# A higher rank for the softplus of stick breaking in a two-layer hybrid trunk

## The chip, the cores and the metric

The kernel runs on one core of one Trainium2 chip. The metric is the device time of one execution in microseconds (us); the time before is the median of three runs. A profile of one more execution gives the start and the duration of every instruction.

## The reference, cut

A trunk of two layers on 512 tokens of 1024 features, in f32. Each layer normalises its input, projects it with one wide matrix, runs five attention branches on pieces of the projection, gates and merges their outputs, projects once more and adds the residual. The branch that the change touches is stick breaking, four heads of 64:

```python
def _stick_breaking_attention(q, k, v):
    ...
        z = jnp.einsum('bqhd,bshd->bhqs', q_blk, k).astype(jnp.float32) * scale
        strict = (s_pos[None, :] < t[:, None])[None, None]
        log_keep = jnp.where(strict, jax.nn.log_sigmoid(-z), 0.0)
        later = lax.cumsum(log_keep, axis=3, reverse=True) - log_keep
        a = jnp.where(strict, jnp.exp(jax.nn.log_sigmoid(z) + later), 0.0).astype(v.dtype)
        return jnp.einsum('bhqs,bshd->bqhd', a, v)
```

The logarithm of the sigmoid of −z is minus the softplus of z, so the kernel forms softplus(z) = max(z, 0) + ln(1 + exp(−|z|)) for every pair of positions, sums it over later keys and subtracts the sum from z before one last exponential. The other branches: sparse attention with an index score and a top-k (A), forgetting attention (B), native sparse attention (D) and attention into 256 memory tokens (E).

## The kernel before, in words

Features lie on the 128 partitions, tokens along the free axis. TensorE (PE) computes every f32 product as three products of split numbers: `split` (lines 291 to 295) makes a high part `hi` by a copy on ScalarE (ACT) and the rest `lo` by a subtraction on VectorE (DVE), and `mm3` multiplies hi·hi, hi·lo and lo·hi. A projection of 128 output features over 512 tokens takes 24 matmuls into one bank `pj`. Its weights come in pieces of 128 x 1024 numbers: `load` has SyncE (SP) fetch one into `wraw` (two buffers), `wload` splits it into `whi` (line 294, ACT) and `wlo` (line 295, DVE), three buffers each. There are 183 such splits; one piece serves one projection.

The order of the work: Python generators are interleaved by `weave`, which gives every instruction a place in the program. When the kernel is built, a scheduler sets each engine's list: of the instructions that its own model of the time takes to be ready it picks the one of the highest rank. The rank is the place in the program, less an offset where the code stands in `tc.high_priority(offset=...)`. Loads and splits of weights stand in `early()`, with an offset of 3000; everything else of the stages told of here had none. On the chip every engine runs its list in order and waits at an instruction until what it needs is there.

Stick breaking is `sb_attn(pr)` (line 1005), called in each layer for two pairs of heads. A pair has two heads `e` and four blocks of keys `j` = 3, 2, 1, 0 with 128, 256, 384 and 512 columns of queries, so there are 8 passes per call and 32 in all. One pass is:

- `begin`: two matmuls of `Ks` and `Qs` and a mask of `sbm` form z in a PSUM bank `sbz` (tag "T" for even `j`, "S" for odd; the index scores `S` use "S" too). ACT makes |z| (line 1030), its exponential and the logarithm of one more (`lnexp`, line 428); DVE makes `sp_t` = max(z, 0) + that (line 1033).
- `middle`, of the pass before: matmuls with `nones` and `ntri` (matrices of −1, full and triangular) add the sums of softplus of later keys into the bank of z: `nones` for later blocks, `ntri` for the block itself, each for the high and the low half of `sp`. They write over what line 1033 reads. Then ACT forms `sb_a`, the last exponential.
- `store`: DVE puts `sp_t` as a high half (line 1049, CAST) and a low half (line 1050, TENSOR_TENSOR) into `sp`.

After the 8 passes 16 products of `sb_a` and the values fill a bank `Yc` (PE). `sb_attn(0)` is woven with the projections for the silu gate of this branch, the index keys and the memory (lines 1458 and 1462); `sb_attn(1)` (line 1465) with the memory queries, the index scores of branch A (`S`, `R` on line 930, `score` on line 931, `Qi` on lines 920 and 921), the gate of branch E (`G`, `Z`) and the first two parts of branch D's projections. Behind it comes the memory attention, woven with merges and the top-k of `score` (lines 976 and 977). In the profiled execution layer 0's two calls lie at about 56 to 98 and 107 to 152 us, layer 1's at 696 to 751 and 758 to 803 us.

Of the kernel before, what the change touches and what calls it, by code (L numbers as in the profile page):

```python
# [14 lines left out]
AF = mybir.ActivationFunctionType  # L15
OP = mybir.AluOpType
# [173 lines left out]
def trunk(ctx: ExitStack, tc: tile.TileContext, xt, memt, pos, wall, small, vec, ca, cb, out):  # L190
    nc = tc.nc
    dep_info = mybir.DependencyInfo(mybir.DependencyClass.NoSync, mybir.DependencyReason.DATA)

    def after(ins, *earlier):
        for e in earlier:
            if e is not None:
                tc.add_manual_dep(ins.ins, e.ins.name, dep_info, reason="issue order")
# [13 lines left out]
    def slot(name, dt=F32, shape=(128, 512)):  # L211
        return st.tile(list(shape), dt, name=name, tag="st")

    def bank(name, tag, shape=(128, 512)):
        return ps.tile(list(shape), F32, name=name, tag=tag, bufs={"pj": 3, "S": 2, "T": 3}[tag])
# [40 lines left out]
    ones1 = const.tile([128, 1], F32, name="ones1")  # L256
# [22 lines left out]
    def mm(out_, lhsT, rhs, start, stop, **kw):  # L279
        return nc.tensor.matmul(out_, lhsT, rhs, start=start, stop=stop, **kw)  # L280
# [10 lines left out]
    def split(raw, hi, lo, scale=None):  # L291

        if scale is None:
            nc.scalar.activation(hi, raw, AF.Copy)  # L294
            nc.vector.tensor_sub(lo, raw, hi.bitcast(F32))  # L295
        else:
            nc.scalar.activation(hi, raw, AF.Copy, scale=scale)
            nc.vector.scalar_tensor_tensor(lo, raw, scale, hi.bitcast(F32), op0=OP.mult, op1=OP.subtract)
# [128 lines left out]
    def lnexp(*a, **k):  # L427
        i = nc.scalar.activation(*a, **k)
        after(i, state["set"])
        state["ln"].append(i)  # L430
        return i
# [57 lines left out]
    f32 = lambda ap: ap.bitcast(F32)  # L489
# [188 lines left out]
    def y_tiles():  # L678
        a = wk.tile([128, 2, T], F32R, name="yhi", tag="yhi", bufs=2)
        b = wk.tile([128, 2, T], F32R, name="ylo", tag="ylo", bufs=2)  # L680
        return a, b
# [63 lines left out]
    def layer(l, xs, begin):  # L745
# [259 lines left out]
        def sb_attn(pr):  # L1005
            SPW = [512, 384, 256, 256]
            if pr == 0:
                sp = big.tile([128, 6, T], F32R, name="sp", tag="xa")
                lv.SP = [[sp[:, 2 * min(j, 2) + s, 256 * (j == 3):256 * (j == 3) + SPW[j]] for s in range(2)] for j in range(4)]
                for s in range(2):  # L1010
                    nc.vector.memset(f32(lv.SP[3][s][:, 0:128]), 0.0)
            SP = lv.SP
            out = {}

            held = wk.tile([128, 1280], F32, name="sb_a", tag="sb_a", bufs=1)
            first_a = [held[:, 0:512], held[:, 512:896], held[:, 896:1152], held[:, 1152:1280]]

            def begin(e, j):

                h = 2 * pr + e  # L1020
                n, w = SPW[j], T - 128 * j
                ks = slice(128 * j, 128 * j + 128)
                z = bank("sbz", "S" if j % 2 else "T")[:, :n]
                mm(z, lv.KC[h][:, ks], lv.QC[h][:, T - n:], True, False)
                mm(z, lv.KlC[h][:, ks], lv.QC[h][:, T - n:], False, False)
                mw = n - w + 128
                mm(z[:, :mw], identb, sbm[:, 256 - mw:], False, True)
                zw = z[:, n - w:]
                t = wk.tile([128, T], F32, name="sp_t", tag="P", bufs=4)[:, :w]
                nc.scalar.activation(t, zw, AF.Abs)  # L1030
                lnexp(t, t, AF.Exp, scale=-1.0)
                lnexp(t, t, AF.Ln, bias=ones1)
                nc.vector.scalar_tensor_tensor(t, zw, 0.0, t, op0=OP.max, op1=OP.add)
                return e, j, z, t

            def middle(e, j, z, t):

                n = SPW[j]
                for jj in range(3, j - 1, -1):
                    for s in range(2):  # L1040
                        mm(z[:, n - SPW[jj]:], ntri if jj == j else nones, SP[jj][s], False, jj == j and s == 1, skip_group_check=True)
                w = T - 128 * j
                a = first_a[j] if e == 0 else wk.tile([128, T], F32, name="sb_a", tag="PT", bufs=5)[:, :w]
                lnexp(a, z[:, n - w:], AF.Exp)
                out[e, j] = a

            def store(e, j, z, t):
                shi, slo = (x[:, SPW[j] - (T - 128 * j):] for x in SP[j])
                nc.vector.tensor_copy(shi, t)
                nc.vector.tensor_sub(slo, t, f32(shi))  # L1050

            one = None
            for e in range(2):
                for j in (3, 2, 1, 0):
                    new = begin(e, j)
                    if one:
                        middle(*one)
                    store(*new)
                    one = new
                    yield  # L1060
            middle(*one)

            Y = bank("Yc", "T")
            last = None
            for j in (0, 1, 2, 3):
                for e in (1, 0):
                    h = 2 * pr + e
                    m = mm(Y[64 * e:64 * e + 64, 128 * j:], lv.VC[:, j, 64 * h:64 * h + 64], out[e, j], j == 0, j == 3, skip_group_check=True)
                    after(m, last)
                    last = m  # L1070
            if pr == 0:
                lv.YC = y_tiles()
            y = slot("yC")
            nc.vector.tensor_mul(y, Y, lv.ZC[0][:, pr])
            split(y, lv.YC[0][:, pr], lv.YC[1][:, pr])
# [433 lines left out]
```

## Time and profile before

| what | value |
|---|---|
| runs before | 1328.40, 1328.65, 1328.89 us; median 1328.65 |
| the profiled execution's own time | 1326.02 us |
| its span, first to last instruction | 1324.2 us |
| granted clock of TensorE, mean of the span | 0.998 |
| busy: PE / DVE / ACT / POOL | 98% / 69% / 51% / 3% |
| instructions | 18915 |
| chain that ended last | PE 70%, DVE 6%, ACT 5%, issue 2% of the span |
| one `whi` (x183) / one `wlo` (x183), mean | 1058 / 1222 ns |
| line 1033, shortest / median / longest of 32 | 277 / 486 / 694 ns |
| line 1050, shortest / median / longest of 32 | 283 / 487 / 694 ns |

"Busy" is the time in which an engine has at least one instruction running; instructions overlap at their ends, so the time from one start to the next is often shorter than a duration. The chain that ended last is followed backwards from the last instruction, at each step to what released it. A wait in brackets behind a row is idle time of the engine just before that instruction, with the releaser.

### The profile page before, as it was taken

What the parts mean: (1) busy time and instruction counts of PE and PEld (TensorE: products, weight loads), DVE (VectorE), ACT (ScalarE), POOL (GpSimd) and SP (SyncE); (2) the same over time, 40 slices, a digit from 0 to 9 for tenths busy, and PEclk for the clock granted to TensorE, in tenths of its full rate; (3) what the DMA queues carried; (4) which work ended last, traced back from release to release, by engine and by line L of the source; (5) the groups of instructions that cost most, each with busy time, mean ns of one, the idle gap of its engine ahead of it and who ended that gap; (6) DMA issues with size and microseconds to landing.
All of it is one profiled execution on the core that took longest, in us unless ns stands there. A gap on an engine that the chain in (4) does not pass through costs nothing.

```text
span 1324.2 us, 18915 instructions
## 1 busy us (share of the span) xinstructions
PE 1300.6 (98%) x7171; PEld 1064.8 (80%) x7171; DVE 914.0 (69%) x1969; ACT 678.2 (51%) x1269; POOL 41.8 (3%) x60
## 2 busy tenths in 40 slices
PE   9999999999999999999999999999999999999997
PEld 7777787887888888888887777778878878888897
DVE  7987999777755556545567699996686564564554
ACT  7877835356544434434447695534484453343341
POOL 0000111000000000000000001110000000000000
PEclk9999999999999999999999999999999999999999
DMA  6442322222222222134523313212122222223231
GB/s 225 135 144 64 117 83 63 90 66 74 72 80 89 79 80 70 58 112 133 181 84 127 97 63 128 80 64 96 48 89 64 87 81 76 86 78 112 96 112 64
DMA packets 40523, 124.10 MB, mean 94 GB/s; under 512 B 4464, under 2 KB 6512, under 8 KB 40432
## 3 DMA queue, kind: packets, MB, share of 16 engines
q1 hardware_dynamic: 40288, 122.63, 28.4%
q8 instruction: 56, 0.92, 0.3%
q10 hardware_dynamic: 144, 0.26, 0.1%
q14 instruction: 35, 0.29, 0.1%
HBM read 118.16 MB, written 4.72 MB: 93 GB/s over the span
## 4 chain that ended last, share of the span: by engine, by line
PE 70%; DVE 6%; ACT 5%; issue 2%; DMA 1%; POOL 0%; DVEq 0%; ACTq 0%
PE pj L280 59%; PE Y L280 4%; PE S L280 3%; PE pt L596 3%; ACT whi L294 1%; DVE wlo L295 1%; DMA mraw<-in_memt_dram 1%; DMA wraw<-in_wall_dram 1%; ACT sw L470 1%; DVE score L977 1%; ACT sw L471 0%; PE sbz L280 0%; DVE m L976 0%; ACT Qi L920 0%; DVE rt L473 0%
## 5 line engine op out<-in xcount | busy, mean ns | idle before, releaser
L280 PE MATMUL pj<-h_hi,whi 128*128 128x512 f32 x1088 | 432.3, 398 | 1.3 <-DVE rt L473 1.0
L280 PE MATMUL pj<-h_lo,whi 128*128 128x512 f32 x1088 | 428.5, 394 | 0.0
L280 PE MATMUL pj<-h_hi,wlo 128*128 128x512 f32 x1088 | 428.1, 394 | 0.0
L294 ACT ACTIVATE whi<-wraw 128x1024 fp32r<-128x1024 f32 x183 | 193.5, 1058 | 333.8 <-PE pj L280 170.3
L295 DVE TENSOR_TENSOR wlo<-wraw,whi 128x1024 fp32r<-128x1024 f32 x183 | 223.6, 1222 | 190.1 <-ACT whi L294 171.5
L280 PEld LDWEIGHTS pj<-h_hi,wlo 128*128 128x128 f32 x1088 | 204.4, 188 | 46.6 <-DVE wlo L295 3.5
L280 PEld LDWEIGHTS pj<-h_hi,whi 128*128 128x128 f32 x1088 | 204.5, 188 | 43.2 <-issue 1.8
L280 PEld LDWEIGHTS pj<-h_lo,whi 128*128 128x128 f32 x1088 | 204.7, 188 | 41.3 <-issue 2.6
L587 ACT ACTIVATE P<-P,nm 128x128 f32<-128x128 f32 (+3 forms) x128 | 71.5, 559 | 77.7 <-DVE nm L586 77.1
L280 PE MATMUL pj<-yhi,whi 128*128 128x512 f32 (+1 forms) x192 | 72.5, 377 | 1.3 <-ACT whi L294 0.5
L586 DVE CUSTOM_DVE_ANT_0 P<-S,CA 128x128 f32<-128x128 f32 (+3 forms) x104 | 48.4, 470 | 36.1 <-PE S L280 35.8
L280 PE MATMUL pj<-ylo,whi 128*128 128x512 f32 (+1 forms) x192 | 71.9, 374 | 0.3 <-DVE ylo L295 0.3
L280 PE MATMUL pj<-yhi,wlo 128*128 128x512 f32 (+1 forms) x192 | 71.9, 374 | 0.0
L596 PE MATMUL pt<-CA,P 128*128 128x128 f32 x384 | 60.2, 274 | 1.7 <-DVE P L635 1.4
L596 PEld LDWEIGHTS pt<-CA,P 128*128 128x128 f32 x384 | 45.6, 141 | 13.0 <-issue 5.2
L434 ACT ACTIVATE G<-pj 128x512 f32<-128x512 f32 x92 | 53.7, 584 | 1.9 <-PE pj L280 1.7
L977 DVE MATCH_REPLACE8 score<-m,score 128x256 f32<-128x256 f32 (+2 forms) x96 | 51.5, 541 | 0.0
L280 PE MATMUL S<-Ks,Qs 128*128 128x256 f32 (+2 forms) x160 | 49.3, 346 | 0.9 <-DVE nm L586 0.9
L976 DVE MAX8 m<-score 128x8 f32<-128x256 f32 (+2 forms) x96 | 49.8, 546 | 0.0
L871 DVE SCALAR_TENSOR_TENSOR G<-G,pj 128x512 f32<-128x512 f32 x64 | 43.6, 681 | 1.3 <-PE pj L280 0.7
L872 DVE TENSOR_TENSOR acc<-acc,G 128x512 f32<-128x512 f32 x64 | 44.0, 687 | 0.7
L280 PEld LDWEIGHTS pj<-yhi,whi 128*128 128x128 f32 x192 | 36.1, 188 | 9.2 <-ACT yhi L294 1.3
(339 smaller groups left out, 2033.2 us busy)
## 6 DMA issues: line engine op xcount, KB each, us to landing
wraw<-in_wall_dram SPq DMA_DIRECT2D x190, 512.0 KB, 3.6
wc<-in_wall_dram SPq DMA_DIRECT2D x16, 256.0 KB, 5.8
x<-in_xt_dram SPq DMA_DIRECT2D x8, 256.0 KB, 5.1
mraw<-in_memt_dram SPq DMA_DIRECT2D x4, 512.0 KB, 4.3
xo<-in_xt_dram SPq DMA_DIRECT2D x8, 256.0 KB, 4.2
xspill<-xn SPq DMA_DIRECT2D x8, 256.0 KB, 2.0
xo<-xspill SPq DMA_DIRECT2D x8, 256.0 KB, 3.1
out_dram<-o SPq DMA_DIRECT2D x8, 256.0 KB, 2.1
```

Of the source, the lines that this page charges most:

```text
L280: return nc.tensor.matmul(out_, lhsT, rhs, start=start, stop=stop, **kw)
L294: nc.scalar.activation(hi, raw, AF.Copy)
L295: nc.vector.tensor_sub(lo, raw, hi.bitcast(F32))
L434: i = nc.scalar.activation(*a, **k)
L470: nc.scalar.activation(sw[a], p[b], AF.Copy)
L586: nc.vector.tensor_tensor_reduce(P, S, mask, -1.0, 3e38, OP.add, OP.min, nm)
L587: nc.scalar.activation(P, P, AF.Exp, bias=nm, scale=-1.0, accum_out=sums)
L596: nc.tensor.transpose(pt[:, 128 * j:128 * j + 128], x[:, c:c + 128], ident)
L871: nc.vector.scalar_tensor_tensor(G, G, gc, p, op0=gop, op1=OP.mult)
L872: nc.vector.tensor_add(acc, acc, G)
L976: nc.vector.max(m8, lv.work[i])
L977: nc.vector.match_replace(lv.work[i], m8, lv.work[i], REPL)
```

## The change

Five instructions of each pass get an offset of 6000, above the 3000 of the weight splits: the exponential and the logarithm on ACT, and lines 1033, 1049 and 1050 on DVE (1034, 1051 and 1052 in the changed file). |z|, `sb_a` and all matmuls keep their rank.

```diff
                 nc.scalar.activation(t, zw, AF.Abs)
-                lnexp(t, t, AF.Exp, scale=-1.0)
-                lnexp(t, t, AF.Ln, bias=ones1)
-                nc.vector.scalar_tensor_tensor(t, zw, 0.0, t, op0=OP.max, op1=OP.add)
+                with tc.high_priority(offset=6000):
+                    lnexp(t, t, AF.Exp, scale=-1.0)
+                    lnexp(t, t, AF.Ln, bias=ones1)
+                    nc.vector.scalar_tensor_tensor(t, zw, 0.0, t, op0=OP.max, op1=OP.add)
...
                 shi, slo = (x[:, SPW[j] - (T - 128 * j):] for x in SP[j])
-                nc.vector.tensor_copy(shi, t)
-                nc.vector.tensor_sub(slo, t, f32(shi))
+                with tc.high_priority(offset=6000):
+                    nc.vector.tensor_copy(shi, t)
+                    nc.vector.tensor_sub(slo, t, f32(shi))
```

No instruction is added or removed, and the lists of SP and POOL are the same as before. The lists of PE, DVE and ACT change in layer 0's two calls and in layer 1's second; in layer 1's first PE's list stays and a few neighbours on ACT and DVE swap. In the stage behind each second call (the memory attention) some of DVE's and PE's rows shift as well. Three places follow. The numbers in names are the program's buffers.

ACT, layer 1, `sb_attn(0)`, the pass of 512 columns (`sp_t_6750`), before:

```order
L428 ACTIVATE sp_t_6750<-sp_t_6750 128x512
L294 ACTIVATE whi_6917<-wraw_6915 128x1024
L517 ACTIVATE Ks_6735<-pj_6709 64x512
L518 ACTIVATE Ks_6735<-pj_6709 64x512
L428 ACTIVATE sp_t_6750<-sp_t_6750,ones1_114 128x512
```

and with the change:

```order
L428 ACTIVATE sp_t_6750<-sp_t_6750 128x512
L294 ACTIVATE whi_6917<-wraw_6915 128x1024
L428 ACTIVATE sp_t_6750<-sp_t_6750,ones1_114 128x512
L517 ACTIVATE Ks_6735<-pj_6709 64x512
L518 ACTIVATE Ks_6735<-pj_6709 64x512
```

The logarithm went from behind two copies to `Ks` to ahead of them; the split of weights stays ahead of it.

DVE, layer 1, `sb_attn(1)`, from the cast of a pass of 512 columns (`sp_t_7268`) to the cast of the next of 128 (`sp_t_7326`), before:

```order
L1049 CAST sp_6548<-sp_t_7268 128x512
L921 TENSOR_TENSOR Qi_7302<-rt1_7204,qhi_7209 32x512
L1050 TENSOR_TENSOR sp_6548<-sp_t_7268,sp_6548 128x512
L463 SCALAR_TENSOR_TENSOR Z_7345<-G_7377,pj_7352 128x512
L931 SCALAR_TENSOR_TENSOR score1_7227<-R_7309,wI_6804,score1_7227 128x256
L931 SCALAR_TENSOR_TENSOR score2_7228<-R_7314,wI_6804,score2_7228 128x384
L934 TENSOR_TENSOR score1_7227<-score1_7227,CA_111 128x128
L295 TENSOR_TENSOR wlo_7628<-wraw_7625,whi_7627 128x1024
L931 SCALAR_TENSOR_TENSOR score3_7229<-R_7319,wI_6804,score3_7229 128x512
L1033 SCALAR_TENSOR_TENSOR sp_t_7326<-sbz_7322,sp_t_7326 128x128
L934 TENSOR_TENSOR score2_7228<-score2_7228,CA_111 128x128
L1049 CAST sp_6548<-sp_t_7326 128x128
```

and with the change:

```order
L1051 CAST sp_6548<-sp_t_7268 128x512
L295 TENSOR_TENSOR wlo_7628<-wraw_7625,whi_7627 128x1024
L1052 TENSOR_TENSOR sp_6548<-sp_t_7268,sp_6548 128x512
L931 SCALAR_TENSOR_TENSOR score1_7227<-R_7309,wI_6804,score1_7227 128x256
L931 SCALAR_TENSOR_TENSOR score2_7228<-R_7314,wI_6804,score2_7228 128x384
L931 SCALAR_TENSOR_TENSOR score3_7229<-R_7319,wI_6804,score3_7229 128x512
L934 TENSOR_TENSOR score1_7227<-score1_7227,CA_111 128x128
L934 TENSOR_TENSOR score2_7228<-score2_7228,CA_111 128x128
L1034 SCALAR_TENSOR_TENSOR sp_t_7326<-sbz_7322,sp_t_7326 128x128
L934 TENSOR_TENSOR score3_7229<-score3_7229,CA_111 128x128
L1051 CAST sp_6548<-sp_t_7326 128x128
```

The split `wlo_7628` went ahead of the low half of `sp` of 512 columns, `Z_7345` behind the cast of 128 columns, and a `Qi` ahead of the stretch.

PE at the same place, before: from the mask of `sbz_7433` to the triangle matmuls of `sbz_7322`, the pass of 128 columns (in a bank of 256):

```order
L280 MATMUL sbz_7433<-sbm_124,identb_123 128x128
L280 MATMUL pj_7514<-h_lo_6455,whi_7510 128x512
L280 MATMUL pj_7514<-h_hi_6454,wlo_7511 128x512
L280 MATMUL pj_7514<-h_hi_6454,whi_7510 128x512
L280 MATMUL pj_7514<-h_lo_6455,whi_7510 128x512
L280 MATMUL pj_7514<-h_hi_6454,wlo_7511 128x512
L280 MATMUL pj_7514<-h_hi_6454,whi_7510 128x512
L280 MATMUL pj_7514<-h_lo_6455,whi_7510 128x512
L280 MATMUL pj_7514<-h_hi_6454,wlo_7511 128x512
L280 MATMUL sbz_7322<-sp_6548,ntri_125 128x256
L280 MATMUL pj_7514<-h_hi_6454,whi_7510 128x512
L280 MATMUL sbz_7322<-sp_6548,ntri_125 128x256
```

and with the change, from the first triangle matmul of `sbz_7264` (512 columns) to the same end:

```order
L280 MATMUL sbz_7264<-sp_6548,ntri_125 128x512
L280 MATMUL sbz_7554<-Qs_6544,Ks_6737 128x512
L280 LDWEIGHTS identb_123
L280 MATMUL sbz_7554<-sbm_124,identb_123 128x128
L280 MATMUL sbz_7433<-Qs_6544,Ks_6735 128x384
L280 MATMUL sbz_7433<-Qs_6544,Ks_6737 128x384
L280 MATMUL sbz_7264<-sp_6548,ntri_125 128x512
L280 LDWEIGHTS identb_123
L280 MATMUL sbz_7433<-sbm_124,identb_123 128x128
L280 MATMUL sbz_7322<-sp_6548,ntri_125 128x256
L280 MATMUL pj_7514<-h_hi_6454,whi_7510 128x512
L280 MATMUL sbz_7322<-sp_6548,ntri_125 128x256
```

The matmuls of `pj_7514` that stood ahead of `sbz_7322`'s first triangle matmul stand behind it; `sbz_7554`, the next pass of 512 columns, is formed earlier.

## Rows read from the trace of the kernel before

**Rows 1.** The page, busy time, share of the span and instructions of each engine
```profile
PE 1300.6 (98%) x7171; PEld 1064.8 (80%) x7171; DVE 914.0 (69%) x1969; ACT 678.2 (51%) x1269; POOL 41.8 (3%) x60
```

**Rows 2.** Waits of PE: what waited <- for what: us in total, times, longest
```profile
PE sbz L280 <- DVE sp_t L1033: 2.5, 4, 1.1
...
PE sbz L280 <- DVE sp L1050: 0.5, 1, 0.5
```

**Rows 3.** Busy time by stretch: stretch, length, PE, PEld, DVE, ACT, POOL, clock, DMA
```profile
56.00:98.00 42.00, 39.85 (x244) 32.65 (x243) 35.42 (x78) 33.30 (x72) 0.00 (x0) 1.00 0.38 122
107.00:152.00 45.00, 44.42 (x216) 33.21 (x215) 42.05 (x79) 42.01 (x79) 0.00 (x0) 1.00 0.19 60
696.00:751.00 55.00, 52.35 (x299) 43.18 (x299) 40.68 (x76) 39.90 (x80) 0.00 (x0) 1.00 0.39 125
758.00:803.00 45.00, 44.43 (x216) 33.23 (x215) 41.97 (x79) 41.95 (x79) 0.00 (x0) 1.00 0.19 59
```

**Rows 4.** Timeline of ACT, layer 1, `sb_attn(0)`: start, us, engine, line, operation
```profile
721.78 0.59 ACT L517 ACTIVATE Ks<-pj 64x512 fp32r<-64x512 f32 x1
...
722.88 0.71 ACT L428 ACTIVATE sp_t<-sp_t,ones 128x512 f32<-128x512 f32 x1
```

**Rows 5.** Timeline of DVE, the same stretch
```profile
721.79 1.22 DVE L295 TENSOR_TENSOR wlo<-wraw,whi 128x1024 fp32r<-128x1024 f32 x1 [1.73 <-ACT whi L294]
723.04 0.69 DVE L496 TENSOR_TENSOR Ks<-pj,Ks 64x512 fp32r<-64x512 f32 x1
723.77 0.69 DVE L1033 SCALAR_TENSOR_TENSOR sp_t<-sbz,sp_t 128x512 f32<-128x512 f32 x1
```

**Rows 6.** Timeline of PE, the same stretch, the wait before it in brackets
```profile
724.52 1.09 PE L280 MATMUL sbz<-sp,nones 128*128 128x256 f32 x6 [1.07 <-DVE sp_t L1033]
```

**Rows 7.** Timeline of PE, layer 0, `sb_attn(0)`, three of its waits
```profile
85.79 0.51 PE L280 MATMUL sbz<-sp,nones 128*128 128x256 f32 x2 [0.53 <-DVE sp_t L1033]
...
87.41 0.39 PE L280 MATMUL pj<-wlo,yhi 128*128 128x256 f32 x1 [0.34 <-DVE wlo L295]
...
95.23 2.38 PE L280 MATMUL Yc<-sb_a,VC 128*64 128x512 f32 x16 [0.42 <-ACT sb_a L428]
```

**Rows 8.** Timeline of DVE, layer 1, `sb_attn(1)`
```profile
780.31 0.68 DVE L1033 SCALAR_TENSOR_TENSOR sp_t<-sbz,sp_t 128x512 f32<-128x512 f32 x1
...
781.57 0.42 DVE L1049 CAST sp<-sp_t 128x512 fp32r<-128x512 f32 x1
782.02 0.69 DVE L921 TENSOR_TENSOR Qi<-rt,qhi 32x512 fp32r<-32x512 f32 x1
...
783.35 0.68 DVE L463 SCALAR_TENSOR_TENSOR Z<-G,pj 128x512 f32<-128x512 f32 x1
...
786.90 0.29 DVE L1033 SCALAR_TENSOR_TENSOR sp_t<-sbz,sp_t 128x128 f32<-128x128 f32 x1
...
787.31 0.22 DVE L1049 CAST sp<-sp_t 128x128 fp32r<-128x128 f32 x1
```

**Rows 9.** Timeline of ACT, the same stretch
```profile
778.92 0.74 ACT L428 ACTIVATE sp_t<-sp_t,ones 128x512 f32<-128x512 f32 x1
...
783.25 0.77 ACT L930 ACTIVATE R<-S 128x256 f32<-128x256 f32 x2 [0.66 <-PE S L280]
...
786.42 0.44 ACT L428 ACTIVATE sp_t<-sp_t,ones 128x128 f32<-128x128 f32 x1
```

**Rows 10.** Timeline of PE, the same stretch
```profile
781.05 1.09 PE L280 MATMUL sbz<-sp,nones 128*128 128x256 f32 x6
781.98 0.40 PE L280 MATMUL pj<-h_lo,whi 128*128 128x512 f32 x1
782.21 0.40 PE L280 MATMUL sbz<-sp,ntri 128*128 128x512 f32 x1
```

**Rows 11.** Timeline of PE, end of layer 1's `sb_attn(1)` and behind it
```profile
794.54 0.39 PE L280 MATMUL S<-KE,Qs 128*128 128x256 f32 x1 [0.25 <-ACT sb_a L428]
...
804.88 0.50 PE L280 MATMUL pj<-h_hi,whi 128*128 128x512 f32 x1 [0.50 <-DVE rt L473]
```

## Prediction

> **What bounds the kernel now.** I read the page first. TensorE (PE) has matmuls running in 1300.6 of 1324.2 us [rows 1], so at most 23.6 us can come from waits, over the whole program. Second, the waits of PE by what they wait for: matmuls into `sbz` stood 2.5 us in four waits for the softplus' last step (`sp_t`, line 1033) and 0.5 us in one for the low half of its stored result (`sp`, line 1050) [rows 2]. These 3.0 us are all that the trace charges directly to the chain that the change raises. Third, the busy time of each engine in the four stretches in which stick breaking runs [rows 3]. They split in two kinds. In the two that weave `sb_attn(0)` with projections PE is idle for 42.00 − 39.85 = 2.15 us (layer 0) and 55.00 − 52.35 = 2.65 us (layer 1), and the two helpers have room (DVE 35.4 of 42 and 40.7 of 55). In the two that weave `sb_attn(1)` PE is idle for only 0.58 and 0.57 us, but DVE and ACT are busy 42.0 of 45 us each: they are almost as full as PE. Removing every idle moment in all four gives 2.15 + 2.65 + 0.58 + 0.57 = 5.95 us; that is the ceiling of any gain made there, 0.45% of the time. Last I read the single rows around the waits, and set the new order beside them.
>
> What can be told from no change is 0.2%, or 2.66 us of 1328.65. The rows come from one execution of 1326.02 us, 2.63 us under the median of the runs shown; I make the sum against it and add 2.63 at the end.
>
> **The change, part by part.** No instruction is added or removed, DMA issues and the orders of SP and POOL stay, so every gain or loss is a wait of PE that goes or comes.
>
> *Layer 1, `sb_attn(0)*: its one long wait, 1.07 us at 724.52 [rows 6]. ACT's new list puts the Ln ahead of two copies to `Ks`. From 721.78 to 722.88 [rows 4] it so comes 1.1 us earlier, and DVE could do `sp_t` at about 722.5. But DVE is in a weight split, `wlo`, from 721.79 to 723.01 [rows 5], which still stands ahead of `sp_t`. So `sp_t` starts at 723.02 in place of 723.77, and the matmuls that clear it 0.75 us earlier. It passes the low half of a `Ks` (0.69 us), which runs behind it now; but the DVE instructions up to the low half of `sp`, for which the next matmuls (`ntri`) wait, are in sum the same as before. The wait moves to them. Bounds: a gain of 1.07 if nothing is late next, nothing if DVE's sum alone decides. I take a gain of 0.1, near the lower bound, because it is their sum that ends last.
>
> The Trainium skill speaks the other way here: Perfetto Trace Analysis, section Optimization Strategy, says to find the gaps on the engine to be kept busy, see which semaphore they wait for, and make that dependency start sooner or end faster, which is what this edit does. By it the 3.0 us of rows 2 would go; by the rows above one third of them goes from one instruction to the next.
>
> *Layer 0, `sb_attn(0)`*: here are waits of 0.53 for `sp_t`, 0.42 for the last exponential ahead of `Yc`, and 0.34 for a `wlo` [rows 7]. The low half of the 384 columns and the `sp_t` of 512 now run ahead of that `wlo`: it comes later by `sp_t` (0.68), the cast (0.42) and that low half (three quarters of some 0.7, 0.5 as an estimate by width) [rows 8], 1.6 us. Bounds: 0.95 gained, 1.6 lost if all of it is a wait. PE's list also moved its uses back, and I take 0, between the two.
>
> *`sb_attn(1)`, both layers*: the term that decides. The stretches of layer 0 and layer 1 are the same to 0.01 us [rows 3] and their lists change alike, so I cost layer 1's and count it twice. In the list of before, eight matmuls of a projection in a row (`pj_7514`, 0.23 us each by the spacing of two starts [rows 10]) stand ahead of the triangle matmuls `ntri` of `sbz_7322`, and before these four others of it. In the new list none is left between the `nones` of `sbz_7264` and these `ntri`: the projection begins behind the first of them. What stays in between is six `nones` (0.93 us to the next start) and about 4350 columns of other matmuls into `sbz` and one into `S`, at 0.23 us for 512, some 1.9 us; 2.8 us in all. The helpers need longer for what these `ntri` wait for, the cast of `sp` with 128 columns:
> - On DVE, before: from `sp_t` 512 at 780.31 to the cast's end at 787.31 + 0.22 = 787.53, 7.22 us. Of that one `Qi` (0.69) and one `Z` (0.68) move out, and one step over 128 columns (as long as `sp_t` 128, 0.29) moves in [rows 8]. 7.22 − 0.69 − 0.68 + 0.29 = 6.1 us. The `wlo` (1.22 [rows 5]) stays inside, and moves ahead of the low half of `sp` 512.
> - On ACT, before: from the Ln of 512 columns at 778.92 to the end of the Ln of 128 columns at 786.42 + 0.44 = 786.86, 7.94 us, with 0.66 idle [rows 9]. In the new list the same instructions stand there but for one Exp of a gate and one Abs less and one copy of 32 rows more; I count 0.2 less for the one that is gone in sum. Without the idle time 7.94 − 0.66 − 0.2 = 7.1 us. Then come `sp_t` 128 and its cast on DVE, 0.41 + 0.22 [rows 8]: the cast ends 7.7 us after that Ln's start.
>
> The `nones` start when the Ln (0.74 [rows 9]) and `sp_t` (0.68 [rows 8]) are through (they write over what it reads), 1.4 us after the Ln's start; PE reaches the `ntri` at 1.4 + 2.8 = 4.2. By ACT it waits 7.7 − 4.2 = 3.5 us; by DVE alone 0.74 + 6.1 − 4.2 = 2.6. I take ACT's, as `sp_t` 128 can't run before that Ln.
>
> Against it: the projection's matmuls are not lost, they stand later and cover later waits. Those are 0.25 at 794.54 and 0.50 at 804.88 [rows 11]. A Yc that comes sooner by what is raised gains at most that much more. 3.5 − 0.25 − 0.50 is 2.75; I take 2.5, the same with a little gained early in the stretch, where raised Ln and `sp_t` pass copies. Bounds per layer: a gain of 0.57, all that is idle there [rows 3], and a loss of 3.5 and one more `wlo` (1.22 [rows 5]) ahead of a projection, 4.7.
>
> Elsewhere the lists differ by a few neighbours, most in the memory attention behind (DVE's passes of the top-k shift); I cost that at nothing, since PE's own list there has merge projections between what it waits for. Without that cover one such swap costs the longer of the two, a split of 1.22 us.
>
> **Sum.** −0.1 + 0 + 2 × 2.5 = +4.9 us; 1326.02 + 4.9 = 1330.9, and against the median 1328.65 + 4.9 = 1333.5 us.
>
> **Rivals.**
> *The waits go, faster (chance 0.16).* Mechanism: the raised Ln and `sp_t` of `sbz_7264` come so much earlier against PE's list that the 7 us of helpers' work lie under the projection ahead of the `nones`, and not behind it. It decides at one point: that `sp_t` must end over 3.5 us before PE gets to the `nones`. Then the 3.0 us of rows 2 and part of the idle of rows 3 are gained: 1328.65 − 3.0 = 1325.6, and no lower than 1328.65 − 5.95 = 1322.7. For it: these instructions are ranked over everything else that the helpers do. Against: ACT has one idle moment of 0.66 in 7.9 us [rows 9], so an earlier Ln puts off the copies to `R`, for which PE waits too.
> *The wait only moves, no change (0.27).* As at 724.52: the gain of one instruction is the delay of its neighbour, and the projections moved back cover as much later as they lose now. 1328.65 + 0 to 2: 1329. For it: at 794 to 805 there are waits to be covered [rows 11]. Against: those that are left sum to 0.75.
> *Splits come late as well (0.07).* Each time a Ln with its Exp, or `sp_t` and its cast (0.68 + 0.42), pass a `whi` or a `wlo`, PE's projection could wait for it. With the bound of 4.7 in both layers: 1328.65 + 9.4 = 1338.0. Only 0.34 of such a wait is in the rows of before [rows 7].
> That the edit does nothing is out: PE's list changes in all of `sb_attn(1)` and in layer 0's `sb_attn(0)`.
>
> **How the numbers follow.** The forecast, a loss in both `sb_attn(1)`, has 0.50: the arithmetic of 7.7 against 4.2 us leaves room, but it rests on durations of one order used in another. Its own range is from 2 × 1.75 to 2 × 3.5 more, 1332.1 to 1335.7. Slower by over 0.2%: 0.50 + 0.07 = 0.57; the same: 0.27; faster: 0.16. The range leaves out the gains past 0.2% (below 1326, 0.16) and what lies over 1338 (about 0.04): 1326 to 1338.
>
> **What would show it.** In the profile after: a wait of PE of 2 to 3 us in front of `sbz<-sp,ntri` of 256 columns at about 785 and again some 651 us earlier, put down to DVE's cast or to `sp_t`; PE idle in the two `sb_attn(1)` stretches up from 0.57 to about 3 us; at layer 1's 724 the wait for `sp_t` gone or under 0.4, and one for `sp` (line 1050, now 1052) in its place; the wait at 804.88 gone. The prediction is wrong if PE's idle time in `sb_attn(1)` stays under 1 us, or if the time lost lies in another stage.

## The result and the profile after

The changed kernel took 1334.89 us (median of six runs, 1333.97 to 1338.24), the kernel before 1328.51 in the same comparison: a ratio of 1.0058 with a 95% interval of 1.0048 to 1.0068. It is slower, by 6.4 us between the medians; 1333.5 was forecast, within 1326 to 1338.

The page of the profiled execution after (1335.23 us, span 1333.4), busy time and share of the span of each engine:

```profile
PE 1305.2 (98%) x7171; PEld 1068.5 (80%) x7171; DVE 913.7 (69%) x1969; ACT 677.9 (51%) x1269; POOL 44.7 (3%) x60
```

The work is the same, in 9.2 us more span [rows 1]. Of these 9.2 us 2.5 are due to the profiled execution of before, which took 1326.02 us and so lay that much under its median of 1328.51; the lags below are larger than the 6.4 us between the medians for the same reason. PE is "busy" 4.6 us longer with the same 7171 matmuls: some of them ran longer, of which more below. The waits of PE in the changed kernel (what waited, for what, us in total, times, longest):

```profile
PE sbz L280 <- DVE sp L1051: 4.3, 2, 2.2
PE pj L280 <- ACT yhi L294: 1.8, 3, 0.7
PE sbz L280 <- DVE sp_t L1034: 1.5, 3, 0.8
...
PE sbz L280 <- DVE sp L1052: 1.1, 3, 0.7
```

Line 1051 is the cast, which stood in no row of before's waits [rows 2]: two waits of 2.2 us each. The busy time of the two stretches that hold `sb_attn(1)` now (stretch, length, PE, PEld, DVE, ACT, POOL, clock, DMA share, GB/s):

```profile
107.00:156.00 49.00, 46.20 (x218) 34.77 (x217) 43.23 (x82) 43.18 (x83) 0.00 (x0) 0.97 0.19 63
...
764.00:814.00 50.00, 47.31 (x222) 35.57 (x221) 45.44 (x88) 44.39 (x85) 0.68 (x1) 0.97 0.17 53
```

PE is idle for 2.80 and 2.69 us in them, against 0.58 and 0.57 [rows 3]. And the mean granted clock in them is 0.97, not 1.00. The place in layer 1, PE's timeline:

```profile
788.28 1.09 PE L280 MATMUL sbz<-sp,nones 128*128 128x256 f32 x6
...
790.05 0.47 PE L280 MATMUL sbz<-sp,ntri 128*128 128x512 f32 x1
...
791.21 0.40 PE L280 MATMUL sbz<-sp,ntri 128*128 128x512 f32 x1
791.45 0.23 PE L280 MATMUL sbz<-sbm,identb 128*128 128x128 bf16 x1
793.83 0.56 PE L280 MATMUL sbz<-sp,ntri 128*128 128x256 f32 x1 [2.15 <-DVE sp L1051]
794.43 0.79 PE L280 MATMUL pj<-h_hi,whi 128*128 128x512 f32 x1
795.02 0.41 PE L280 MATMUL sbz<-sp,ntri 128*128 128x256 f32 x1
795.23 0.63 PE L280 MATMUL pj<-h_lo,whi 128*128 128x512 f32 x1
795.66 0.63 PE L280 MATMUL pj<-h_hi,wlo 128*128 128x512 f32 x1
```

and DVE's and ACT's in the same stretch, from the end of the logarithm of 512 columns to the cast of 128:

```profile
786.81 0.69 DVE L921 TENSOR_TENSOR Qi<-rt,qhi 32x512 fp32r<-32x512 f32 x1
787.53 0.69 DVE L1034 SCALAR_TENSOR_TENSOR sp_t<-sbz,sp_t 128x512 f32<-128x512 f32 x1
...
789.14 1.22 DVE L295 TENSOR_TENSOR wlo<-wraw,whi 128x1024 fp32r<-128x1024 f32 x1
790.27 0.68 DVE L1052 TENSOR_TENSOR sp<-sp_t,sp 128x512 fp32r<-128x512 f32 x1
...
793.15 0.29 DVE L1034 SCALAR_TENSOR_TENSOR sp_t<-sbz,sp_t 128x128 f32<-128x128 f32 x1 [0.20 <-ACT sp_t L428]
...
793.55 0.22 DVE L1051 CAST sp<-sp_t 128x128 fp32r<-128x128 f32 x1
```

```profile
785.97 0.76 ACT L428 ACTIVATE sp_t<-sp_t,ones 128x512 f32<-128x512 f32 x1
...
787.90 1.06 ACT L294 ACTIVATE whi<-wraw 128x1024 fp32r<-128x1024 f32 x1 [0.20 <-PE pj L280]
...
792.72 0.39 ACT L428 ACTIVATE sp_t<-sp_t,ones 128x128 f32<-128x128 f32 x1
```

The arithmetic of the prediction holds in its form; two of its lengths were off. From the Ln's start at 785.97 to the end of the cast (793.55 + 0.22 = 793.77) are 7.8 us (7.7 forecast). PE has its last matmul ahead of the `ntri` at 791.45, 5.5 us after that Ln's start, and stands until 793.83. What bounds the helpers is ACT, as taken: the `sp_t` of 128 columns waits 0.20 us for its Ln. PE came 1.3 us later than the 4.2 forecast: 0.9 because the `nones` started at 788.28 and not at 787.4 (DVE had a `Qi` of 0.69 between the Ln and `sp_t` 512), and the rest between there and 791.45, where 3.2 us went for what I had put at 2.8. With the 0.23 us of that last matmul the wait is 2.15 us in place of 3.5; the missing part stands ahead of it.

That the helpers did not become slower shows when the kernel before is set beside it. There PE came to the same `ntri` at 788.03, without a wait:

```profile
788.03 0.28 PE L280 MATMUL sbz<-sp,ntri 128*128 128x256 f32 x1
```

From the Ln's start at 778.92 [rows 9] to the end of the cast at 787.53 [rows 8] the helpers took 8.6 us; now they take 7.8. But what PE has to do between the start of the `nones` and these `ntri` (its cover, from here on) was 7.0 us before (781.05 [rows 10] to 788.03) and is 3.4 now (788.28 to 791.68). Seventeen matmuls of projections stood in that stretch before; none does now.

The new thing stands behind the wait: the projection's matmuls start 0.43 us apart at 795.23 and 795.66 where before they started 0.23 apart [rows 10]. The granted clock shows why (windows of 2 us):

```profile
792.00:794.00 2.00, 0.17 (x1) 0.17 (x1) 1.80 (x7) 1.98 (x8) 0.00 (x0) 0.97 0.66 211
794.00:796.00 2.00, 1.97 (x5) 1.47 (x6) 2.00 (x6) 1.89 (x6) 0.00 (x0) 0.50 0.00 0
796.00:798.00 2.00, 2.00 (x8) 1.60 (x7) 1.65 (x5) 1.95 (x4) 0.00 (x0) 0.68 0.00 0
```

The clock was at half there, 1.2 in place of 2.4 GHz: (1 − 0.97 + 1 − 0.50 + 1 − 0.68) x 2 = 1.7 us of full clock are missing. That is an estimate of the cost from above; the lags below show how much of it is left farther on. The same sum gives 1.7 at 138 to 142 us (layer 0's `sb_attn(1)`) and 1.7 at 746 to 750 (layer 1's `sb_attn(0)`, behind two waits of 0.81 and 0.68). In the kernel before the clock was full in every window of 2 us but at the end, where PE has nothing left to do.

**Where the time came from.** Both traces have 7171 matmuls, so I compare the start of the matmul with the same number in PE's list, at places where the lists agree. Lag of the changed kernel's profiled execution behind that of before:

| place, us of before | lag, us | added since the row above |
|---|---|---|
| 54, ahead of layer 0's first call | 0.87 | 0.87 (start-up, before any reordered place) |
| 105, behind it | 1.36 | 0.5 (a wait of 0.57 at 56.61 that is not of stick breaking) |
| 200, behind layer 0's second call | 4.69 | 3.3 |
| 690, ahead of layer 1's first call | 4.23 | −0.5 |
| 726, behind the wait of rows 6 | 4.23 | 0.0 |
| 757, behind layer 1's first call | 5.71 | 1.5 |
| 850, behind layer 1's second call | 9.11 | 3.4 |
| 1317, last matmul | 9.06 | 0.0 |

The wait at 56.61 is one of `ssq` for line 382, ahead of the first raised pass. In e2 below, which raises nothing in this call, it is longer still (0.89), and e1, which raises all of this call, has none there, so it belongs to the execution and not to the change. Behind it the first call of layer 0 adds nothing (−0.1).

### The profile page after: what moved, and what is told of

It is laid out like the page before. It is cut to its first block, busy times and chain, and to the rows that moved or that the text cites. A ratio compares the mean times of both kernels' runs of the same rounds, so it can differ in the third digit from the quotient of the medians.

```text
span 1333.4 us, 18921 instructions
## 1 busy us (share of the span) xinstructions
PE 1305.2 (98%) x7171; PEld 1068.5 (80%) x7171; DVE 913.7 (69%) x1969; ACT 677.9 (51%) x1269; POOL 44.7 (3%) x60
## 4 chain that ended last, share of the span: by engine, by line
PE 81%; ACT 7%; DVE 6%; issue 3%; DMA 2%; POOL 0%; SPq 0%; DVEq 0%; ACTq 0%
PE pj L280 68%; PE Y L280 4%; PE S L280 3%; PE pt L596 3%; ACT whi L294 2%; PE sbz L280 1%; DVE wlo L295 1%; ACT Qi L920 1%; ACT sw L470 1%; PE Yc L280 1%; ACT sw L471 1%; DMA mraw<-in_memt_dram 1%; DMA x<-in_xt_dram 1%; PE ssq L280 0%; ACT sp_t L428 0%
## 5 line engine op out<-in xcount | busy, mean ns | idle before, releaser
L294 ACT ACTIVATE whi<-wraw 128x1024 fp32r<-128x1024 f32 x183 | 193.5, 1058 | 346.1 <-PE pj L280 188.0
L1344 POOL TENSOR_SCALAR P<-P,rsum 128x256 f32<-128x256 f32 x32 | 33.7, 1065 | 372.7 <-DVE rsum L670 336.9
```

The costliest lines, as they stand in the source:

```text
L1344: nc.gpsimd.tensor_scalar(x, x, r[:, e:e + 1], None, op0=OP.mult)
```

## The experiments

The first question is whether the loss sits at one place of `sb_attn(1)`, or is spread over the raised passes; the second, what the slow clock costs; the third, whether it matters that the softplus outranks the splits. In all of them lines 1032 to 1034 (Exp, Ln and `sp_t`) and 1051 and 1052 (`store`) of the change stand in `with up(...)`, where `up(c)` gives the offset if c holds and none if not. The kernel before was run beside each batch.

### e1: only the first call of each layer

```diff
-                with tc.high_priority(offset=6000):
+                with up(pr == 0):
```

(at both places)

> Only sb_attn(0) of each layer is raised. Theory A (the loss of sb_attn(1) is one place, where its matmul list lost the projection between the nones of the 512-column pass and the ntri of the next): the waits of 2.2 us and the slow clock behind them in both sb_attn(1) are gone, and what is left is what the changed kernel lost in sb_attn(0): 0.5 us in layer 0 and 1.4 in layer 1, so 1.9 us slower than before (1330.4). Theory B (each raised pass holds up splits and copies a little, wherever it stands): half of the 32 passes, so half of the loss, 3.2 us slower (1331.7).

Measured: 1328.27 us against 1327.72, ratio 1.0009 (0.9999 to 1.0019): no difference that can be told. By the matmuls' starts the first calls cost 0.3 us (layer 0) and 0.9 us (layer 1) in the profiled execution. The interval ends 2.5 us above before: theory A's 1.9 us lie inside, theory B's 3.2 outside. What e1 loses is less than half of the change's 6.4 us, so most of the loss is in the second calls; its profile has no wait for the cast.

### e2: one pass

```diff
-                with tc.high_priority(offset=6000):
+                with up((pr, e, j) == (1, 0, 1)):
```

(at both places)

> A single pass of sb_attn(1) is raised in each layer: first head, 384 columns (e = 0, j = 1). It gives almost the whole list of matmuls of the change in sb_attn(1). Theory A: the wait of about 2.2 us ahead of the ntri of the 128-column pass is there in both layers, and PE idle and clock are as in the changed kernel: 4.5 to 6.5 us slower than before (1333 to 1335). Theory B: 2 of 32 raised passes, 0.4 us slower, not to be told from before.

Measured: 1332.09 us, ratio 1.0033 (1.0020 to 1.0046), 4.4 us slower. Five instructions of one pass per layer, 10 of the 160 that the change raises, give two thirds of its loss. The waits of this kernel:

```profile
PE sbz L280 <- DVE sp L1054: 4.3, 2, 2.2
PE sbz L280 <- DVE sp_t L1037: 2.9, 4, 1.3
```

The same two waits for the cast (in the files of the experiments e1 to e3 `sp_t`, cast and low half are lines 1037, 1054 and 1055; in e4 1040, 1057 and 1058). Its two layers differ, though. Windows of 2 us behind the wait, in layer 0 and in layer 1:

```profile
138.00:140.00 2.00, 2.00 (x8) 1.66 (x9) 2.00 (x7) 1.96 (x5) 0.00 (x0) 0.75 0.00 0
140.00:142.00 2.00, 2.00 (x8) 1.71 (x7) 1.85 (x4) 1.40 (x3) 0.00 (x0) 0.50 0.00 0
...
792.00:794.00 2.00, 1.79 (x8) 1.41 (x9) 2.00 (x6) 1.98 (x6) 0.00 (x0) 1.00 0.00 0
794.00:796.00 2.00, 2.00 (x13) 1.69 (x11) 1.84 (x6) 1.95 (x5) 0.00 (x0) 1.00 0.00 0
```

In layer 0 the clock fell to half behind the wait, in layer 1 it stayed at 1.00 behind one of the same length. The lag added is 3.6 us in layer 0 (from 105 to 200 us of before) and 2.2 in layer 1 (757 to 850). That separates the two costs: the lost cover is 2.2 us, and a fall of the clock adds some 1.3 to it.

### e3: all passes but that one

```diff
-                with tc.high_priority(offset=6000):
+                with up((pr, e, j) != (1, 0, 1)):
```

(at both places)

> All passes are raised but that one (e = 0, j = 1 of sb_attn(1)); eight projection matmuls stand ahead of the ntri of the 128-column pass again. Theory A: no wait over 1 us in sb_attn(1); 0 to 2 us slower than before (1328.5 to 1330.5). Theory B: 30 of 32 of the loss, 6 us slower (1334.5).

Measured: 1328.38 us, ratio 1.0008 (0.9998 to 1.0017). With 150 of 160 instructions raised a loss can no longer be told. All of its waits of PE for stick breaking that the profile lists:

```profile
PE sbz L280 <- DVE sp_t L1037: 1.8, 4, 0.8
...
PE sbz L280 <- DVE sp L1055: 0.9, 2, 0.7
```

None is for the cast, none over 0.8 us. Theory B is out.

### e4: matmuls put into the wait

```diff
+                if (pr, e, j) == (1, 1, 0):
+                    for _ in range(8):
+                        mm(z[:, :512], nones, lv.QC[h][:, T - 512:], True, True)
                 mm(z, lv.KC[h][:, ks], lv.QC[h][:, T - n:], True, False)
```

> The changed kernel with eight more matmuls of 512 columns per layer whose result is overwritten, 0.23 us each, 1.84 us in all, in sb_attn(1) between the nones of the 512-column pass and the ntri of the next, where PE stood idle for 2.2 us; the lists are otherwise those of the change. If the clock that fell to half behind that wait is a cost of its own: the granted clock stays at 1.00 there, the 1.7 us that it cost in each layer come back, and the kernel is 3.4 us faster than the changed one (1331.5) though it does more. If the clock has no part in the loss: as the changed kernel, 1334.9. If the added matmuls come on top: 1338.6.

Measured: 1333.01 us (1331.50 to 1336.28), ratio to before 1.0042 (1.0026 to 1.0058). It does 2 x 1.84 us more work than the changed kernel and is, by the medians, 1.8 us faster than that kernel's 1334.82 in e5 (another batch; the intervals of the two ratios overlap, so the gain isn't certain). In the profiled execution the wait in layer 0 was down to 0.45 us, and the clock full:

```profile
134.20 0.86 PE L280 MATMUL sbz<-Qs,nones 128*128 128x512 f32 x3
...
135.52 1.17 PE L280 MATMUL sbz<-Qs,nones 128*128 128x512 f32 x4
...
137.67 0.39 PE L280 MATMUL sbz<-sp,ntri 128*128 128x256 f32 x1 [0.45 <-DVE sp L1057]
```

```profile
138.00:140.00 2.00, 1.79 (x10) 1.50 (x10) 2.00 (x7) 1.98 (x5) 0.00 (x0) 1.00 0.00 0
140.00:142.00 2.00, 2.00 (x13) 1.68 (x12) 1.84 (x6) 1.95 (x5) 0.00 (x0) 1.00 0.00 0
```

No window of 2 us before the end of this execution has a clock under 0.99. By the starts of the other matmuls the lag added is 2.2 us in either second call, as in layer 1 of e2 where the clock held: the added work went into the wait and cost nothing there. One full clock in a profile proves little, since it also held in places without the fill (e2's layer 1). The runs say more: the mean clocks of these five are 0.995 to 0.998, four of them 0.997 or above, and those of the eleven runs of the changed kernel (the comparison and e5) are 0.993 to 0.996. That speaks for fewer falls of the clock with the fill, though e2, without it, has 0.996 to 0.997. The gain over the change was half of the 3.4 forecast, and the run at 0.995 took 1336.28: the fill does not exclude a fall.

### e5: the change again

> The changed kernel as it is, on the chip of this batch, for its scatter and for comparison: 5 to 8 us slower than before (ratio 1.004 to 1.006). If the slow clock behind the waits comes in some executions only, its time goes with its mean granted clock: about 1.3 us (a thousandth of the span) for each 0.001.

Measured: 1334.82 us, ratio 1.0052 (1.0038 to 1.0065). The times of its runs follow the clock only loosely: 1334.2 at 0.996, 1334.9 on average at 0.995, 1334.4 at 0.994 and 1336.3 at 0.993, less than the 1.3 us expected for each 0.001. The profiled execution shows the rest: the clock was at half for longer in layer 0 than in the first profile, and full in layer 1, behind the same wait of 2.2 us:

```profile
138.00:140.00 2.00, 1.90 (x5) 1.42 (x6) 2.00 (x6) 1.92 (x6) 0.00 (x0) 0.50 0.00 0
140.00:142.00 2.00, 2.00 (x7) 1.61 (x6) 1.66 (x6) 1.93 (x4) 0.00 (x0) 0.50 0.00 0
142.00:144.00 2.00, 2.00 (x8) 1.61 (x7) 2.00 (x4) 0.43 (x1) 0.00 (x0) 0.50 0.00 0
...
794.00:796.00 2.00, 1.50 (x6) 1.20 (x7) 2.00 (x7) 2.00 (x6) 0.00 (x0) 1.00 0.01 4
796.00:798.00 2.00, 2.00 (x12) 1.71 (x11) 1.84 (x6) 1.93 (x5) 0.00 (x0) 1.00 0.00 0
```

The lag added is 4.7 us in layer 0's second call and 2.3 in layer 1's. So the cover costs 2.3, and the clock 0 or 2.4 here, 1.0 to 1.1 in either layer in the execution of the first profile. Which of the waits is followed by a fall changes from execution to execution.

### e6: above all but the splits

```diff
-                with tc.high_priority(offset=6000):
+                with tc.high_priority(offset=1500):
```

(at both places)

> Offset 1500 in place of 6000: the softplus ranks above all else but below the weight splits (3000). The lists are nearly those of the change (2 of PE's rows, 4 of ACT's and 8 of DVE's lines differ). If what costs is that splits of weights come later, as they rank below the softplus: the time of before, 1328. If it is the order against the rest (copies of the index stage and the keys, and through the scheduler the projections): as the changed kernel, 5 to 8 us slower than before.

Measured: 1334.04 us, ratio 1.0048 (1.0035 to 1.0060): the changed kernel's time, with its two waits of 2.2 us for the cast. Behind both the clock stayed full in its profile, and the lag added by the second calls is 2.2 and 2.3 us. That the softplus outranks the splits of weights, which the offset of 6000 gives it, has next to no part in what the edit does. What counts is the rank against everything else.

### e7: without the store

```diff
-                with tc.high_priority(offset=6000):
-                    nc.vector.tensor_copy(shi, t)
-                    nc.vector.tensor_sub(slo, t, f32(shi))
+                nc.vector.tensor_copy(shi, t)
+                nc.vector.tensor_sub(slo, t, f32(shi))
```

> Exp, Ln and the last step of the softplus raised in all passes, cast and low half not. The list keeps eight projection matmuls ahead of the ntri of the 128-column pass. Theory (the lost cover there is the loss): no wait over 1 us in sb_attn(1), 0 to 2 us slower than before. Rival (the raised ACT instructions hold up the copies and splits, whatever PE's list): 5 us slower.

Measured: 1328.79 us, ratio 1.0009 (1.0000 to 1.0017). The raised Exp, Ln and `sp_t` alone keep the cover ahead of that `ntri`, and don't cost what the change costs. There is no wait over 1 us in `sb_attn(1)`; the longest one for stick breaking, 1.5 us, stands in layer 1's first call. The two halves of the edit are not additive: raising the store alone leaves all of PE's list as it was before (shown by the list that is built; no run was made of it), and only both together take the cover away.

### e8: the first half, in one pass

```diff
-                with tc.high_priority(offset=6000):
+                with up((pr, e, j) == (1, 0, 1)):
                     lnexp(t, t, AF.Exp, scale=-1.0)
```

(and the store as before the change)

> Exp, Ln and the last step raised in one pass of sb_attn(1) alone (first head, 384 columns). In the changed kernel the stretch of sb_attn(1) up to that pass gained 0.4 us in each layer, by the starts of PE's matmuls, before the loss began. If this part can be had alone: 0.8 us faster than before (1327), under what can be told by 0.2%; if it comes back as a later wait: no difference.

Measured: 1327.11 against 1327.68 us, ratio 0.9993 (0.9984 to 1.0002). The early gain is there at 140 us in layer 0 (lag −0.6, 0.4 less than at 105) and at 784 in layer 1 (0.3 less than at 757), but by the last matmul the lag is +0.1. Not to be told from before; no version here beats it.

## Why the prediction was right, and where it was off

**The main term, `sb_attn(1)`, was right in place and mechanism; that its size came out so close is in part luck.** Forecast: 2.5 us per layer, from a wait at the `ntri` of 128 columns. Shown: the waits come when the cover is lost (e2, e6) and are absent when it is kept (e3, e7), and where the clock held they cost 2.2 (e2, layer 1), 2.3 (e5, layer 1) and 2.2 and 2.3 (the two layers of e6). But 2.5 was a wait of 3.5 less 1.0 that was to be won back around it. The wait was 2.15, and next to nothing of it was won back; the two errors cancel but for 0.3 us. What was not luck: the sum was made on the list of each engine and not on the waits of before. Of 3.0 us of waits [rows 2] there was little to be gained, and the loss came from a place that had no wait at all. (The two stretches that I took to be the same to 0.01 us are so for PE alone; DVE and ACT differ by up to 0.08 [rows 3]. Nothing hangs on it.)

**The offset against waits behind did not come.** The wait at 804.88 [rows 11] went, as forecast; but behind each second call PE now waits 0.7 us for `yhi` instead (two of the three waits above; before there was one, of 0.4, in the whole program), which I had left at nothing.

**Layer 1, `sb_attn(0)`: −0.1 was forecast for the wait at 724.52 [rows 6], and 0.0 came.** In the changed kernel it is two waits, as forecast:

```profile
728.02 1.09 PE L280 MATMUL sbz<-sp,nones 128*128 128x256 f32 x6 [0.26 <-DVE sp_t L1034]
...
729.93 0.50 PE L280 MATMUL sbz<-sp,ntri 128*128 128x512 f32 x1 [0.23 <-DVE sp L1052]
```

The wait for `sp_t` fell to 0.26, one for line 1052 came. But some 15 us on, the reordered helpers cost what I had put at nothing. Waits of PE of 0.81 and 0.68 us stand there for the pass of 256 columns, where before there were 0.33 (at 739.07) and 0.55 (at 740.33):

```profile
744.07 0.50 PE L280 MATMUL sbz<-sp,nones 128*128 128x256 f32 x2 [0.81 <-DVE sp_t L1034]
...
745.47 0.39 PE L280 MATMUL sbz<-sp,ntri 128*128 128x256 f32 x1 [0.68 <-DVE sp L1052]
```

With and without a fall of the clock the call added 1.5 and 0.5 us (first profile, e5). Layer 0's `sb_attn(0)`, put at 0, added 0.5 and 0.7 in the same two executions; without the time up to and with the wait at 56 us it is −0.1 and 0.4, and e2, where this call is unchanged, scatters by as much. So the 0 is not refuted.

**What the sum lacked is the clock.** The profile's clock row of before was full everywhere, and I took it as given, with 4.9 us as the sum. The medians moved by 6.4 and, in e5, 7.1. Where the clock held, the traces give 2 x 2.3 for the second calls and about 0.5 for layer 1's first, 5.1. What is left, 1.3 to 2.0, is of the size that falls of the clock give: none to 2.4 us for each wait of 2.2, by execution. That it is the clock in the median run as well is argued and not shown, as only the profiled executions tell where it fell. A stall on PE was priced as its own length, and it can cost the work behind it, too: behind a wait of 2.2 us in e5's layer 0 the windows show 0.50. The Trainium skill (TensorE: Matmul & The Clock Gate, section HAM oscillation — how this bites in real kernels) has this for a wait that is long enough: the array's clock falls to half, and the work behind it starts slow. The traces agree with the fall, but behind waits shorter than those of the page's example, and not each time: the clock stayed at 1.00 behind the same wait in e5's layer 1.

**The rivals.** "The waits go" is out: `sp_t` 512 ended at 788.22, just ahead of the `nones` at 788.28, where that rival needed over 3.5 us. "The wait only moves" holds for the place at 724 alone. "Splits come late as well" is out as the cause: e6 keeps the splits first and is as slow.

What stays open: why the build's scheduler, given one pass of 384 columns a higher rank, moves the projection behind the `ntri`. e2, e3 and e7 show that it takes the raise of both halves of that pass; how its model of the time leads there is not known. Nor was it tried to keep the change and hold the projection ahead by hand.

## What to carry to other kernels

Where a scheduler sets the order at build time, a rank is not a local edit: five instructions of one pass took seventeen matmuls of projections out of a stretch elsewhere and made two thirds of the loss. Read the new list of the engine that bounds the kernel first, find what no longer stands between a producer and its reader, and set the helpers' time in between against the work that is left. A wait that is absent from the profile of before because it is covered is the one that a reordering can bring.

## What was not expected of the hardware

Behind a wait of 2.2 us TensorE's granted clock fell to half in some executions and not in others, with the same kernel and in the same place: it fell behind four of the eight such waits in the profiles of the changed kernel (two), e2 and e6. A fall took 1.7 us of full clock out of the windows behind it (first profile) or 3.4 (e5's layer 0: 0.96, three windows of 0.50 and one of 0.84); by the lags it cost less, 1.0 to 1.3 and 2.4 us. In the first profile and in e6 the clock fell also at 744 to 750 us, behind two waits, neither over 0.81 us; five other profiles have nearly the same two waits (0.79 to 0.80 and 0.68 us) and no fall there. The kernel before, with waits up to 1.4 us, was at full clock in its profiled execution until PE's last work was done.
